# Two transformer layers in split float32: the split weights in one tile, with the token-major pairs 128 bytes further on

## The chip, the cores and the metric

The kernel runs on 1 core of a Trainium2 chip. The metric is the device time of one execution in microseconds (us). Three runs of the kernel before took 845.11 to 846.7 us, median 845.73.

## The reference

Two post-norm layers work on `x` of 256 tokens by 1024 channels, all in float32. Cut to what matters:

```python
def hybrid_mixer(x, ...):
    proj = jnp.einsum('bsd,de->bse', x, w_in)          # 12 parts side by side
    y_a = sliding_window_attention(a_q, a_k, a_v, sinks, slopes_a)
    y_b = gated_short_conv(b_h, b_b, b_c, conv_w)
    y_c = moba_attention(c_q, c_k, c_v, slopes_c)
    merged = (sigmoid(g_a) * (y_a @ w_br_a) + sigmoid(g_b) * (y_b @ w_br_b)
              + sigmoid(g_c) * (y_c @ w_br_c))
    return merged @ w_out

def reference(x, ...):
    for l in range(2):
        x = layer_norm(ALPHA * x + hybrid_mixer(x, ...), ln1_g[l], ln1_b[l])
        ffn = (silu(x @ w_gate) * (x @ w_up)) @ w_down
        x = layer_norm(ALPHA * x + ffn, ln2_g[l], ln2_b[l])
    return x
```

## The kernel before, in words

**Split arithmetic.** Every matrix product is made of three matmuls on numbers split in two: a high part, which is the value rounded to the type `float32r`, and a low part, which is what is left. High times high, high times low and low times high are added up in PSUM. ScalarE writes the high part (`wh`) and VectorE subtracts to get the low part (`wl`); for weights this is `parts` (L182 and L183 in the profile), for activations the helper `halve` (L272 and L273).

**Pieces and the ring.** The host packs all weights into 140 pieces of 128 partitions by 2048 columns (8 KB per partition, 1 MB). `load` (L154) brings a piece into one of three raw buffers on SP's queue. `open_splits` gives it a place and `split_piece` adds its split, two parts of 1024 columns. The place is one of four slots of a ring, a tile for `wh` and a tile for `wl` from the pool `wts`, which is taken in turn; three pieces of a layer's cycle go into a tile that stands free at that moment, `wA` or `wB` (the table `place`). `take` makes the planner finish a piece's split in its order of emission, `drop` gives the slot back.

**Two orders of operands.** In a matmul one operand stands still in the array (it is loaded by a LDWEIGHTS) and the other moves through it.
- `whole` works on a block of 256 output channels in channel-major order: `trio` lets the weights stand still (128 x 128) and moves 256 tokens of `xx` past them. A piece is two accumulators `acc` of 24 matmuls. `branch` (`br`) and `merge` (`gc`) use `trio` in the same way, `br` with `y` instead of `xx`.
- `half_pair` works on two pieces for half of the tokens in token-major order: `tokens` lets 128 tokens of `xx` stand still and moves 256 weight columns past them (two runs of 128 columns, 4 KB apart). Its accumulators are `hp`, 24 matmuls per piece and half, 48 per pair and half. It is used where the tokens of one half are ready before those of the other: around a norm. Its pieces are 2 and 3 of layer 0 (`qkv_pair`), the first four of the FFN in each layer (`ffn_pair`), and the first four of layer 1 (`qkv_pair`).
- `project` (`pr`, mostly 512 columns) and `cv` move weights too, in runs of 512 columns.

**Addresses.** All big tiles start at a multiple of 256 bytes in their partition, also `wh`, `wl`, `mx` and the hidden tiles. `xx` and `y` start 48 words (192 bytes) further on (`AHEAD`), and every slice of them that a matmul reads keeps this remainder. So does a small tile of 16 words behind each, which brings the next tile back to a multiple of 256.

**Order.** A planner (`Plan`) emits the work of ScalarE and VectorE in the order of its estimated times, while the loops emit TensorE's. Engines PE, DVE, ACT and SP keep the order of emission. The order in a layer is: q, k and v blocks; attention in eight rounds, between blocks of the other projections, each round with scores (`s`), transposes (`tp`) and mixing (`yp`); `branch`, `merge`; the output projection with the first norm, in whose shadow the pairs of the FFN run; 18 blocks of the FFN (`whole`, 864 matmuls); the down projection with the second norm, in whose shadow the pairs of the next layer run.

```python
def tokens(acc, wv, k, h, src, first, last):
    wh, wl = wv
    t = slice(h * P, (h + 1) * P)
    mm(acc, src[k][:, 0, t], wh, first, False)
    mm(acc, src[k][:, 0, t], wl, False, False)
    mm(acc, src[k][:, 1, t], wh, False, last)

def trio(acc, wh, wl, src, first, last):
    mm(acc, wh, src[:, 0, :], first, False)
    mm(acc, wh, src[:, 1, :], False, False)
    mm(acc, wl, src[:, 0, :], False, last)
```

Of the kernel before, what the change touches and what calls it, by code (L numbers as in the profile page):

```python
# [9 lines left out]
FT = mybir.dt.float32  # L10
FR = mybir.dt.float32r
# [5 lines left out]
P = 128  # L17
D = 1024
S = 256
L = 2  # L20
KD = D // P
# [3 lines left out]
PIECE = 2048  # L25
CHUNK = 1024
RING = 4
RAWS = 3
N_IN, N_BR, N_OUT, N_FF, N_DN = 27, 6, 4, NF, NF // 2
PER_LAYER = N_IN + N_BR + N_OUT + N_FF + N_DN  # L30
# [3 lines left out]
FAR = 1.0e30  # L34
LINE = 64
EARLY = 8
AHEAD = 48


# [77 lines left out]
def trunk(ctx: ExitStack, tc: tile.TileContext, x, first, w, sinks, conv, ln, out):  # L117
    nc = tc.nc
    pool = lambda name, bufs, **k: ctx.enter_context(tc.tile_pool(name=name, bufs=bufs, **k))
    const = pool("const", 1)  # L120
    raws = pool("raws", RAWS)
    wts = pool("wts", RING)
    keep = pool("keep", 1)
    work = pool("work", 2)
    ps = pool("ps", 4, space=bass.MemoryType.PSUM)
    ctx.enter_context(tc.manual_schedule(engines={ENG.PE, ENG.DVE, ENG.Activation, ENG.SP}))
# [3 lines left out]
    place = {}  # L130
# [4 lines left out]
    total = L * PER_LAYER  # L135
    slots = [0.0] * RING
    spare, ready, chunks, raw, landed, rawfree = {}, {}, {}, {}, {}, {}
    pos = {"load": 0, "split": 0, "take": 0}

    def cut(j):  # L140
# [3 lines left out]
    def load(hold=False):  # L144
        j = pos["load"]
        if j >= total:
            return
        pos["load"] += 1
        if j:
            raw[j] = raws.tile([P, PIECE], FT, name="raw")  # L150
            if hold:
                nc.vector.memset(raw[j][:, 0:1], 0.0)
            for s in cut(j):
                nc.sync.dma_start(raw[j][:, s], w[j - 1][:, s])  # L154
        landed[j] = max(landed.get(j - 1, 3.5), rawfree.get(j - RAWS, 0.0) + 2.0) + 3.0
        open_splits()
# [4 lines left out]
    def open_splits():  # L161
        while pos["split"] < pos["load"]:
            j = pos["split"]
            if j in place:
                if place[j] not in spare:
                    return
                t = spare.pop(place[j])
                both = keep.tile([P, 2, PIECE], FR, tag=place[j], name="w" + place[j])
                ready[j] = both[:, 0, :], both[:, 1, :]
            else:  # L170
                if not slots:
                    return
                t = slots.pop(0)
                ready[j] = wts.tile([P, PIECE], FR, name="wh"), wts.tile([P, PIECE], FR, name="wl")
            pos["split"] += 1
            if j:
                split_piece(j, max(t, landed[j]))
# [7 lines left out]
    def split_piece(j, t, n=CHUNK):  # L185
        def last(task):
            rawfree[j] = task.ready
            load()

        need = T.pe + 5.2 * (j - pos["take"])  # L190
        ss = [slice(c, c + n) for c in range(0, PIECE, n)]
        chunks[j] = [T.add(parts(j, s), t - (1.5 if len(cut(j)) > 1 and not i else 0.0), max(need - t, 0.0) + 0.001 * i, last if s.stop == PIECE else None)
                     for i, s in enumerate(ss)]

    def take():
        j = pos["take"]
        pos["take"] += 1
        T.run()
        T.finish(*chunks.pop(j))
        return j  # L200

    def drop(j):
        if j in place:
            if j % PER_LAYER == N_IN + N_BR + N_OUT:
                spare["B"] = T.pe
        else:
            slots.append(T.pe)
        del ready[j]
        open_splits()
# [90 lines left out]

    xx = keep.tile([P, AHEAD + KD * 2 * S], FR, name="xx")
    xx = xx[:, AHEAD:].rearrange("p (k a s) -> p k a s", k=KD, a=2)
    xk = [xx[:, k] for k in range(KD)]
    rest = keep.tile([P, LINE - AHEAD], FT, name="rest")
    nc.gpsimd.memset(rest, 0.0)


    both = keep.tile([P, KD, 2 * S], FT, tag="A", name="first")
    rest = keep.tile([P, LINE - AHEAD], FT, name="rest2")
    nc.gpsimd.memset(rest, 0.0)  # L310
# [12 lines left out]
    spin = ps.tile([P, P], FT, tag="o", name="spin")  # L323
    for i in range(EARLY):
        nc.tensor.matmul(spin, idle, idle, start=True, stop=True)
# [292 lines left out]
    def mixer_tiles():  # L618
        mix = keep.tile([P, 18 * S + 4 * (S + 2) + 56], FT, tag="mix", name="mix")
        aq, ak, av, cq, ck, cv = [  # L620
            mix[:, lo * S:hi * S].rearrange("p (k s) -> p k s", k=k)
            for lo, hi, k in ((0, 4, 4), (4, 5, 1), (5, 6, 2), (6, 10, 4), (10, 14, 4), (14, 18, 2))]
        return aq, ak[:, 0, :], av, cq, ck, cv, mix[:, 18 * S:18 * S + 4 * (S + 2)].rearrange("p (k s) -> p k s", k=4)
# [26 lines left out]
    for l in range(L):  # L650
        aq, ak, av, cq, ck, cv, up = tiles = mix or mixer_tiles()
        y = keep.tile([P, AHEAD + 12 * 2 * S], FR, tag="A", name="y")
        y = y[:, AHEAD:].rearrange("p (b k a s) -> p b k a s", b=3, k=4, a=2)
        nc.gpsimd.memset(up[:, :, 0:2], 0.0)
# [39 lines left out]
        for n in range(2):  # L694
            j = take()
# [47 lines left out]
            for part in (conv_h, conv_c, conv_b):  # L743
                whole(part)

        gs = keep.tile([P, 2, KD, S], FT, tag="B", name="gs")
        sums, raw_gates, sig = {}, {}, {}

        def gates(b):
# [66 lines left out]
        merge()  # L816
        spare["A"] = spare["B"] = T.pe
        open_splits()

        hid, last_f = [], {f: [] for f in range(NF)}  # L820
# [127 lines left out]
```

## Time and profile before

| what | value |
|---|---|
| median of three runs | 845.73 us (845.11 to 846.7) |
| the profiled execution | 849.06 us |
| its span, first to last instruction | 847.3 us |
| TensorE busy | 834.6 us, 99% |
| VectorE, ScalarE, GpSimd busy | 583.3, 456.5, 56.9 us |
| mean granted clock of TensorE | 0.997 |
| read from memory | 153.11 MB, 182 GB/s over the span |

The profile shows one execution. A duration of a matmul in it runs from its start to its modelled end, and matmuls overlap (a `hp` matmul lasts some 280 ns while the next starts some 118 ns later), so the rate is not read from mean durations. It is read from the chain of waits, where a row is an unbroken stretch of one kind of matmul with its time and its count.

### The profile page before, as it was taken

To read this page: it belongs to the slowest core of one execution; us is meant where nothing else is said; L and a number is where in the kernel's file an instruction comes from. 1 tells how busy PE (TensorE), PEld (TensorE's weight loads), DVE (VectorE), ACT (ScalarE), POOL (GpSimd) and SP (SyncE) were. 2 spreads that over 40 slices of the span, in tenths; PEclk is the share of its full clock that TensorE was granted. 3 is DMA by queue.
4 is the path that set the end of the run, shared out by engine and by line. 5 is a ranking of instruction groups with operands and counts; after the bars stand their busy time and mean duration, and the time that the engine had idled before them with its cause. 6 is when DMAs were issued, how large, how long until landed. Compare 5 with 4: busy or idle time off the path is not lost.

```text
span 847.3 us, 15513 instructions
## 1 busy us (share of the span) xinstructions
PE 834.6 (99%) x6390; PEld 793.7 (94%) x6390; DVE 583.3 (69%) x980; ACT 456.5 (54%) x809; POOL 56.9 (7%) x81
## 2 busy tenths in 40 slices
PE   8999999999999999999999999999999999999996
PEld 7989989999899999988899899999998999999885
DVE  5588999577967566545657799966688666556435
ACT  6667677645525445434347776865563345444320
POOL 2003500000110000000000044000000100000000
PEclk9999999999999999999999999999999999999998
DMA  8753445556655555556336424554646465555511
GB/s 302 295 186 114 150 153 202 198 196 199 249 199 197 184 174 193 199 191 235 121 107 243 149 100 142 207 209 166 222 161 245 171 224 196 199 172 184 193 50 50
DMA packets 23318, 155.15 MB, mean 183 GB/s; under 512 B 2608, under 2 KB 2896, under 8 KB 5840
## 3 DMA queue, kind: packets, MB, share of 16 engines
q1 hardware_dynamic: 22032, 149.96, 50.1%
q0 software_dynamic: 1216, 4.22, 1.7%
q8 instruction: 50, 0.82, 0.4%
q14 instruction: 20, 0.16, 0.1%
HBM read 153.11 MB, written 1.05 MB: 182 GB/s over the span
## 4 chain that ended last, share of the span: by engine, by line
PE 94%; DMA 3%; DVE 1%; ACT 1%; issue 0%; SPq 0%; POOLq 0%; POOL 0%; DVEq 0%; ACTq 0%
PE acc L254 46%; PE pr L254 17%; PE hp L254 9%; PE br L254 8%; PE gc L254 5%; PE cv L254 3%; PE tp L267 2%; PE s L254 2%; DMA gb<-ln 1%; DMA first<-first 1%; PE yp L490 1%; DMA raw<-w 1%; PE yp L492 0%; DVE xtok L518 0%; ACT xa L272 0%
## 5 line engine op out<-in xcount | busy, mean ns | idle before, releaser
L254 PE MATMUL acc<-xx,wh 128*128 128x256 f32 x2304 | 405.7, 280 | 2.1 <-ACT wh L272 2.1
L183 DVE TENSOR_TENSOR wl<-raw,wh 128x1024 fp32r<-128x1024 f32 x266 | 322.4, 1229 | 108.7 <-ACT wh L182 108.0
L182 ACT ACTIVATE wh<-raw 128x1024 fp32r<-128x1024 f32 x266 | 274.2, 1053 | 194.4 <-PE acc L254 79.6
L254 PEld LDWEIGHTS acc<-xx,wh 128*128 128x128 f32 x2304 | 350.2, 188 | 3.4 <-ACT wh L272 2.6
L254 PE MATMUL acc<-xx,wl 128*128 128x256 f32 x1152 | 321.9, 279 | 0.7 <-DVE wl L273 0.4
L254 PEld LDWEIGHTS acc<-xx,wl 128*128 128x128 f32 x1152 | 218.8, 190 | 1.5 <-DVE wl L273 0.8
L254 PE MATMUL hp<-wh,xx 128*128 128x256 f32 x384 | 70.9, 282 | 0.0
L279 DVE TENSOR_TENSOR g<-g,acc 128x256 f32<-128x256 f32 x72 | 30.1, 418 | 57.5 <-PE acc L254 57.1
L254 PE MATMUL br<-y,wh 128*128 128x256 f32 x384 | 67.9, 281 | 0.0
L254 PE MATMUL pr<-wh,hidA 128*128 128x512 f32 (+1 forms) x216 | 60.7, 366 | 0.0
L254 PEld LDWEIGHTS hp<-wh,xx 128*128 128x128 f32 x384 | 59.6, 188 | 0.0
L254 PEld LDWEIGHTS br<-y,wh 128*128 128x128 f32 x384 | 58.9, 190 | 0.0
L254 PE MATMUL br<-y,wl 128*128 128x256 f32 x192 | 54.0, 281 | 0.0
L254 PE MATMUL hp<-wl,xx 128*128 128x256 f32 x192 | 53.6, 279 | 0.0
L254 PE MATMUL gc<-xx,wh 128*128 128x256 f32 x256 | 45.3, 281 | 0.0
L254 PEld LDWEIGHTS pr<-wh,hidA 128*128 128x128 f32 x216 | 39.1, 189 | 6.6
L254 PE MATMUL pr<-wh,hidB 128*128 128x512 f32 (+1 forms) x144 | 41.8, 366 | 0.0
L254 PE MATMUL pr<-wl,hidA 128*128 128x512 f32 (+1 forms) x108 | 39.5, 366 | 0.0
L254 PEld LDWEIGHTS gc<-xx,wh 128*128 128x128 f32 x256 | 39.3, 190 | 0.0
L254 PEld LDWEIGHTS hp<-wl,xx 128*128 128x128 f32 x192 | 36.1, 188 | 0.0
L254 PEld LDWEIGHTS br<-y,wl 128*128 128x128 f32 x192 | 36.0, 188 | 0.0
L254 PE MATMUL gc<-xx,wl 128*128 128x256 f32 x128 | 36.0, 281 | 0.0
(134 smaller groups left out, 959.5 us busy)
## 6 DMA issues: line engine op xcount, KB each, us to landing
raw<-w SPq DMA_DIRECT2D x136, 1024.0 KB, 5.0
gb<-ln POOLq DMA_DIRECT2D x8, 512.0 KB, 5.1
raw<-w SPq DMA_DIRECT2D x6, 512.0 KB, 8.8
first<-first SPq DMA_DIRECT2D x4, 512.0 KB, 5.7
xtok<-x SPq DMA_DIRECT2D x2, 512.0 KB, 6.3
out<-xtok SPq DMA_DIRECT2D x3, 256.0 KB, 2.0
out<-xtok SPq DMA_DIRECT2D x2, 128.0 KB, 1.8
cw<-conv POOLq DMA_DIRECT2D x1, 12.0 KB, 5.5
```

Of the source, the lines that this page charges most:

```text
L182: return [act(n) + (lambda: nc.scalar.activation(wh[:, s], raw[j][:, s], AF.Copy),), dve(n) + (lambda: nc.vector.tensor_sub(wl[:, s], raw[ ...
L183: dve(n) + (lambda: nc.vector.tensor_sub(wl[:, s], raw[j][:, s], wh[:, s].bitcast(FT)),)]
L254: nc.tensor.matmul(acc, a, b, start=start, stop=stop)
L267: nc.tensor.transpose(tp[:, i, :], src(i), ident)
L279: return [dve(n) + (lambda: nc.vector.tensor_mul(dst, a, b),)]
L490: nc.tensor.matmul(yp[los[a], :], v[:, 0, vsel[a]], pts[a][:, 0:2, :], start=True, stop=False)
```

## The change

The pool `wts` goes. In its place stands one tile `ring` with four slots of 2 x 2048 + 32 words, `wh` and `wl` of a piece side by side in a slot. A counter (`turns`) picks the slot. A piece of the list `pairs`, which are the pieces that `half_pair` reads, starts 32 words (128 bytes) past a multiple of 64 words (256 bytes); all others start at a multiple of 256 bytes. The kept tiles `wA` and `wB` are 64 words longer, so that the first piece of the FFN (in `wB`, a pair) can start 32 words in; `gs`, which shares its memory with `wB`, gets the same length.

```diff
@@ -119,8 +120,8 @@
     raws = pool("raws", RAWS)
-    wts = pool("wts", RING)
     keep = pool("keep", 1)
+    ring = keep.tile([P, RING * (2 * PIECE + HALF)], FR, name="ring")
     work = pool("work", 2)
@@ -135,6 +136,9 @@
     slots = [0.0] * RING
     spare, ready, chunks, raw, landed, rawfree = {}, {}, {}, {}, {}, {}
+    turns = [0]
+    ffn = N_IN + N_BR + N_OUT
+    pairs = [2, 3] + [l * PER_LAYER + j for l in range(L) for j in range(ffn, ffn + 4)] + [PER_LAYER + j for j in range(4)]
     pos = {"load": 0, "split": 0, "take": 0}
@@ -165,13 +169,17 @@
                 t = spare.pop(place[j])
-                both = keep.tile([P, 2, PIECE], FR, tag=place[j], name="w" + place[j])
-                ready[j] = both[:, 0, :], both[:, 1, :]
+                both = keep.tile([P, 2 * PIECE + LINE], FR, tag=place[j], name="w" + place[j])
+                lo = HALF * (j in pairs)
+                ready[j] = both[:, lo:lo + PIECE], both[:, lo + PIECE:lo + 2 * PIECE]
             else:
                 if not slots:
                     return
                 t = slots.pop(0)
-                ready[j] = wts.tile([P, PIECE], FR, name="wh"), wts.tile([P, PIECE], FR, name="wl")
+                lo = turns[0] % RING * (2 * PIECE + HALF)
+                turns[0] += 1
+                lo += (lo % LINE + HALF * (j in pairs)) % LINE
+                ready[j] = ring[:, lo:lo + PIECE], ring[:, lo + PIECE:lo + 2 * PIECE]
@@ -743,7 +751,8 @@
-        gs = keep.tile([P, 2, KD, S], FT, tag="B", name="gs")
+        gs = keep.tile([P, 2 * KD * S + LINE], FT, tag="B", name="gs")
+        gs = gs[:, :2 * KD * S].rearrange("p (b k s) -> p b k s", b=2, k=KD)
```

`HALF` is 32 and `LINE` is 64, in words of 4 bytes. Every engine has the same instructions in the same order in both kernels; only the name of the weights' tile differs (`ring` for `wh` and `wl`). What a split waits for differs: with a tile per slot it waited for the release of the tile, and in one tile it waits for the last instructions that touch its own region.

## Rows read from the trace of the kernel before

**Rows 1.** The page, part 1: busy us, share of the span, instructions
```profile
PE 834.6 (99%) x6390; PEld 793.7 (94%) x6390; DVE 583.3 (69%) x980; ACT 456.5 (54%) x809; POOL 56.9 (7%) x81
```

**Rows 2.** Waits of PE: us in total, times, longest us
```profile
PE acc L254 <- ACT wh L272: 2.1, 2, 1.4
PE spin L325 <- DVE xtok L322: 1.1, 1, 1.1
PE tp L267 <- DVE xtok L518: 0.6, 1, 0.6
PE tp L267 <- DVE prob L455: 0.5, 1, 0.5
PE acc L254 <- DVE wl L273: 0.4, 2, 0.2
PE acc L254 <- DVE raw L152: 0.2, 1, 0.2
```

**Rows 3.** Chain that ended last, `acc`, `br`, `gc`: start us, us, what, count
```profile
34.45 11.31 PE acc L254 x96
...
46.47 4.10 PE acc L254 x36
...
99.70 9.54 PE acc L254 x84
...
157.94 33.92 PE br L254 x288
191.86 22.61 PE gc L254 x192
...
261.34 4.10 PE acc L254 x36
...
265.65 97.52 PE acc L254 x828
...
448.51 1.42 PE acc L254 x12
...
450.25 10.90 PE acc L254 x96
...
461.86 4.10 PE acc L254 x36
...
479.32 5.47 PE acc L254 x48
...
564.44 1.38 PE acc L254 x12
...
681.26 97.52 PE acc L254 x828
```

**Rows 4.** The same chain, the pairs `hp`
```profile
237.17 8.48 PE hp L254 x72
...
246.09 2.83 PE hp L254 x24
...
252.63 5.66 PE hp L254 x48
...
445.78 2.73 PE hp L254 x24
```

**Rows 5.** Stretches: from:to us, length, busy us per engine, PEclk, DMA share, GB/s
```profile
266.00:362.00 96.00, 96.00 (x818) 96.00 (x817) 59.15 (x87) 46.05 (x69) 0.00 (x0) 1.00 0.55 188
446.00:448.00 2.00, 2.00 (x20) 2.00 (x19) 1.79 (x3) 1.88 (x3) 0.00 (x0) 1.00 0.78 254
```

**Rows 6.** Waits of all engines, the two of the weight splits
```profile
DVE wl L183 <- ACT wh L182: 108.0, 86, 5.7
ACT wh L182 <- PE acc L254: 79.6, 38, 2.4
```

**Rows 7.** The page, part 6: a load of a piece, KB each, us to landing
```profile
raw<-w SPq DMA_DIRECT2D x136, 1024.0 KB, 5.0
```

More of the change, by code (lines that the diff above doesn't have):

```diff
@@ L36 @@
 EARLY = 8
+HALF = 32
 AHEAD = 48
```

## The prediction

> **What bounds the kernel now.** I read the page's busy times first. TensorE is busy 834.6 of 847.3 us, and VectorE, ScalarE and GpSimd have slack [rows 1]. TensorE's waits come next: all of them together are 4.9 us [rows 2]. So nothing but TensorE's own pace can be worth much, and the chain of waits, which is 94% TensorE, is read for that pace: each of its rows is an unbroken stretch of matmuls, and its time divided by its count is the time of one.
>
> The reader is to see that one form, 128x256, runs at two paces. The matmuls of whole column blocks (`acc`) take 9.54 / 84 = 113.6 ns in one stretch, 113.9 in the stretch of 36 in front of the FFN loop, and 97.52 / 828 = 117.8 ns in the FFN loop, in both layers [rows 3]. `br` (33.92 / 288) and `gc` (22.61 / 192) take 117.8 [rows 3]. The token-major pairs (`hp`) take 8.48 / 72 = 117.8 and 2.83 / 24 = 117.9, and in one stretch alone 2.73 / 24 = 113.8 [rows 4]. The chain has 17 rows of `hp` with 672 matmuls, and 16 of these rows are at the long pace; of its 39 rows of `acc`, 31 are at 115 ns or less. [...]
>
> The pace is kept for a whole stretch and can differ in the next, with something else between (transposes, scores, the other order of operands): 36 `acc` at 113.9, two transposes, and 828 `acc` at 117.8 [rows 3]. The 828 of a loop pass through all four slots of the ring four times at one pace, so the slot is not the reason either.
>
> **What the addresses are.** In `whole` the weights stand still and start at a multiple of 256 bytes, and `xx` moves and starts 192 past one: the moving operand lies 64 bytes below the stationary one, modulo 256. In the pairs `xx` stands still (192) and the weights move (0): 64 above. The change puts the moving weights of the pairs at 128, which is 64 below 192: the relation that `whole` has now. That relation gives no guarantee, as the FFN loop and `br` and `gc` have it and run at 117.8 [rows 3]. But it is the one in which most stretches settle at the short pace, while in the pairs' present relation one of 17 does.
>
> **The change part by part.** (1) The pairs' addresses. Of the 672 matmuls in the 17 rows, 24 are at the short pace already [rows 4], so 648 can gain 117.8 - 113.6 = 4.2 ns each: 2.7 us if all turn, nothing if none does. All of it lies on TensorE, the bound, with no cover. Which stretches turn? Four of 72 follow a projection or `acc` without transposes between, 288 matmuls; the rest follow 2 to 12 transposes. `acc` has both outcomes behind transposes: two transposes lead to the long pace at 265.65 and at 681.26, three to the short pace at 450.25 [rows 3]. The pairs have 144 matmuls behind two transposes, which I leave at the long pace by that row, and I count four fifths of the other 528, as 31 of 39 rows of `acc` are short: 422, less the 24 that have it, some 400. 400 x 4.2 = **1.7 us gained**. The ends of this term are 0 and 2.7.
>
> (2) What follows the pairs. An `acc` stretch starts in whatever position the pairs leave. 36 `acc` behind long-pace pairs run at 113.9, and 12 `acc` behind the one short-pace stretch at 1.42 / 12 = 118 [rows 3, 4]. These are few: 12, 36, 36 and 12 in the four places, and 96 behind the last of them. Were all 180 now short to turn long, it would cost 0.8 us; were the 12 to turn short, they would give 0.05. I take 0, as the entry from pairs of the same relation has no row. The loops of 828 lie behind two transposes and those 36 `acc`; as long as the 36 stay short, what enters the loop is what enters it now, so I take no change for the loops; the end is 828 x 4.2 = 3.5 us gained for each loop (a rival, below).
>
> (3) The ring as one tile. The same instructions stand on every engine in the same order. What moves is what the splits wait for: a split of 1024 columns waits for the last reader of its own region, where it waited for the last reader of the whole tile. ScalarE's splits now wait 79.6 us for `acc` and VectorE's subtractions 108.0 us for ScalarE, in 38 and 86 waits [rows 6]; these are waits for a slot to come free, with splits a whole ring ahead of TensorE. Releasing the first half of a piece earlier lets a split start up to half a piece earlier, 24 x 0.118 = 2.8 us. TensorE waits for `wh` and `wl` only in the helper's lines L272 and L273, that is for the first block, 2.1 and 0.4 us, before the ring is ever reused [rows 2], so this is worth 0. What it could reach is the 1.1 us that TensorE waits for VectorE in transposes of `xtok` and `prob` [rows 2]: up to 1.1 gained if these vanish, and as much lost if one more appears because a subtraction that waits for a region holds VectorE's queue with a softmax or a norm behind it. I take 0 and keep +-1.1.
>
> (4) The padding (128 bytes more in each slot, 256 in each kept tile) adds no instruction and moves no other tile off its multiple of 256, so 0; a step that reads from the padded tile has the same number of elements. Loads stay 136 of 1 MB, 5.0 us each to land, on SP's queue in the same order [rows 7].
>
> Sum: 1.7 us gained. The profiled execution took 849.06 us with a span of 847.3, so it would take 847.4; the median of the runs, 845.73, stands 3.3 us below it, and the same gain gives **844.0 us**. About 0.2% (1.7 us) is what a measurement of this kernel can tell from no change, so the forecast stands on that border.
>
> [...] What the rows show first: two paces of one form at the full clock [rows 3, 5], so something beside the number of columns sets the pace. [...]
>
> **The rivals.** *A. The address is not what matters* (chance 0.20). The pace is set at the entry of a stretch, by where it falls in time, and the pairs are slow because of what stands before them: transposes and projections, which stay. For it: the `hp` stretch at 445.78 is short at the old address [rows 4], and `acc` is long in 828 at the good one [rows 3]. Against it: 1 of 17 rows against 31 of 39. Then 845.7, give or take the 1.1 of (3).
>
> *B. The FFN loops are carried along* (0.14). The pairs stand right in front of both loops, with 36 `acc` and two transposes between. If another position enters the loop and it settles at the short pace, 828 x 4.2 = 3.5 us more for each: with the forecast's 1.7, 840.5 for one loop and 837.0 for both. For it: 96 `acc` behind three transposes settle short after a long stretch of 12 [rows 3, 4], so what stands before the transposes matters. Against: both layers enter alike today and both come out long.
>
> *C. Short stretches behind the pairs turn long, and it is slower* (0.10). In layer 1 the pairs feed the attention part directly: 96 and 36 `acc` at 450.25 and 461.86, and 624 more up to 566 that run at 113.6 to 115. If the entry changes and all 756 settle long, 756 x 4.2 = 3.2 us lost, and with pairs that gain nothing the time is 848.9. It decides from about 400 matmuls more turned long than short (1.7 / 4.2 ns). Against it: layer 0 enters its attention part at 117.8 (34.45, 11.31 / 96) and layer 1 at 113.5, and behind the first scores both are at 113.9 [rows 3], so the scores and transposes in between seem to wipe out the entry.
>
> **How the numbers follow.** The forecast has 0.56, with 240 to 648 of the pairs turned, 1.0 to 2.7 us: 844.7 to 843.0. It ends over 0.2% faster in a little more than half of its cases (0.33), and within 0.2% in the others (0.23). A is within 0.2% (0.18) but for 0.01 at either side; B is faster (0.14); C is slower in 0.09 and within 0.2% in 0.01. So faster 0.48, same 0.42, slower 0.10. The range reaches down past one loop of B to 839.0 (one loop 3.5, all pairs 2.7, and some of (3)) and leaves out most of the case of both loops; upward it reaches 847.2, half of C, and leaves out the rest.
>
> **What would show it.** In the profile after, the rows of `hp` in the chain should read about 8.2 for 72, 5.45 for 48 and 2.73 for 24, in at least half of their matmuls; the rows of 36 `acc` stay at 4.10 and the loops at 97.52; `br` at 33.92 and `gc` at 22.6; and TensorE's waits stay near 4.9 us. All rows of `hp` at 117.8 would make (1) wrong and A right; a loop at 94.1 us would be B; rows of 84 `acc` at 9.9 instead of 9.54 would be C.

## The result and the profile after

The changed kernel takes 839.39 us (median of 4 runs, 839.11 to 840.19), the kernel before, measured beside it, 846.22 (845.11 to 846.88). The ratio is 0.9916 with a 95% interval of 0.9901 to 0.9932: faster by 0.84%, or 6.8 us. The predicted time was 844.0 us in a range from 839.0 to 847.2, so the time stands just inside its lower end, 0.4 us from it. The profiled execution has a span of 837.7 us, against 847.3 before.

TensorE's busy time answers to [rows 1]: it fell by 7.1 us, most of the 9.6 by which the span fell.

```profile
PE 827.5 (99%) x6390; PEld 787.3 (94%) x6390; DVE 584.6 (70%) x980; ACT 457.7 (55%) x809; POOL 56.8 (7%) x81
```

So the gain is one of pace, and the chain of waits of the changed kernel says where. Its rows (start us, us, what, count) answer to [rows 3, 4]; all these matmuls have the form 128x256.

```profile
33.62 10.90 PE acc L262 x96
...
156.14 33.92 PE br L262 x288
190.06 22.61 PE gc L262 x192
...
235.37 8.48 PE hp L262 x72
...
244.28 2.74 PE hp L262 x24
...
256.61 2.83 PE hp L262 x24
259.44 4.24 PE acc L262 x36
263.90 93.86 PE acc L262 x828
...
428.30 5.46 PE hp L262 x48
...
444.47 11.31 PE acc L262 x96
...
670.82 4.24 PE acc L262 x36
675.28 93.86 PE acc L262 x828
```

Read them against the rows before, by time over count:

| stretch | before, ns each | after, ns each | us in the two layers together |
|---|---|---|---|
| FFN loop, 828 `acc`, both layers | 117.8 | 93.86 / 828 = 113.4 | -7.3 |
| pairs `hp`, 672 | 24 of them short | 168 of them short | -0.6 |
| 36 `acc` ahead of the loop, both layers | 113.9 | 4.24 / 36 = 117.8 | +0.3 |
| 96 `acc` behind the pairs | 117.8 in layer 0, 113.5 in layer 1 | 113.5 and 117.8 | 0 (-0.4 and +0.4) |
| `br` and `gc` | 117.8 | 117.8 | 0 |

These add to -7.6 us. The medians differ by 6.8, with an interval (0.0099 and 0.0068 of 846.2) of 5.8 to 8.4 us. The remaining 2.0 us of the 9.6 between the two spans lie in the start and in single waits that vary from execution to execution: the first run below has the loops, `br` and `gc` at the paces of the kernel before and a span of 845.0, 2.3 us shorter. Some 0.7 of these 2.3 us are a matter of pace too: its first 72 pairs and the 96 `acc` of layer 0 came out short, without any shift. So the -0.4 us of layer 0 in the table is no sign of the change.

The 168 short pairs are the 24 at 244.28, the two rows of 48 at 428.30 and 434.09, and two more rows of 24; none of the four blocks of 72 turned. The pairs, which alone were shifted, gave little. The loops, whose weights stand at multiples of 256 bytes as they did, gave nearly all.

The clock has no part in it: the granted clock reads 1.00 in a stretch of either pace in [rows 5], with TensorE busy throughout. This is the loop of layer 0 after the change by windows (from and to, length, busy us per engine, granted clock, DMA share, GB/s): again 1.00, and TensorE busy 90.00 of 90.00 us, at the other pace.

```profile
266.00:356.00 90.00, 90.00 (x796) 90.00 (x795) 58.95 (x84) 45.30 (x68) 0.00 (x0) 1.00 0.57 199
```

The waits of TensorE answer to [rows 2] (us in total, times, longest).

```profile
PE acc L262 <- ACT ring L280: 1.2, 2, 0.8
```

Those of the weight splits, in the view of all engines, answer to [rows 6].

```profile
DVE ring L191 <- ACT ring L190: 86.4, 49, 5.5
...
ACT ring L190 <- PE pr L262: 51.1, 15, 8.9
```

ScalarE's splits waited 79.6 us for `acc` before; that wait is gone from the view. VectorE's wait for ScalarE fell from 108.0 to 86.4 us. The finer waits of the one tile do what the third step said. TensorE, which waited 2.1 and 0.4 us in all for split weights [rows 2], got next to nothing from it.

### The profile page after: what moved, and what is told of

It is laid out like the page before. It is cut to its first block, busy times and chain, and to the rows that moved or that the text cites. A ratio compares the mean times of both kernels' runs of the same rounds, so it can differ in the third digit from the quotient of the medians.

```text
span 837.7 us, 15533 instructions
## 1 busy us (share of the span) xinstructions
PE 827.5 (99%) x6390; PEld 787.3 (94%) x6390; DVE 584.6 (70%) x980; ACT 457.7 (55%) x809; POOL 56.8 (7%) x81
## 4 chain that ended last, share of the span: by engine, by line
PE 92%; DVE 4%; DMA 1%; POOL 1%; issue 0%; ACT 0%; SPq 0%; POOLq 0%
PE acc L262 43%; PE pr L262 20%; PE hp L262 9%; PE br L262 8%; PE gc L262 5%; PE cv L262 3%; PE tp L275 2%; PE s L262 1%; DMA first<-first 1%; PE yp L498 1%; DVE ring L191 1%; DVE xa L281 1%; PE yp L500 0%; POOL hh L740 0%; DVE prob L467 0%
## 5 line engine op out<-in xcount | busy, mean ns | idle before, releaser
L262 PE MATMUL acc<-xx,ring 128*128 128x256 f32 x3456 | 405.0, 278 | 1.4 <-ACT ring L280 1.2
L262 PEld LDWEIGHTS acc<-xx,ring 128*128 128x128 f32 x3456 | 399.1, 189 | 2.8 <-ACT ring L280 1.7
L191 DVE TENSOR_TENSOR ring<-raw,ring 128x1024 fp32r<-128x1024 f32 x266 | 322.2, 1229 | 87.1 <-ACT ring L190 86.4
L190 ACT ACTIVATE ring<-raw 128x1024 fp32r<-128x1024 f32 x266 | 274.7, 1053 | 104.6 <-PE pr L262 51.1
L262 PE MATMUL hp<-ring,xx 128*128 128x256 f32 x576 | 70.3, 281 | 0.0
L262 PEld LDWEIGHTS hp<-ring,xx 128*128 128x128 f32 x576 | 68.2, 189 | 0.1
L262 PE MATMUL br<-y,ring 128*128 128x256 f32 x576 | 68.2, 281 | 0.0
L262 PEld LDWEIGHTS br<-y,ring 128*128 128x128 f32 x576 | 68.0, 189 | 0.0
L262 PE MATMUL pr<-ring,hidA 128*128 128x512 f32 (+1 forms) x324 | 66.2, 366 | 0.0
L262 PEld LDWEIGHTS pr<-ring,hidA 128*128 128x128 f32 x324 | 55.9, 189 | 9.9
L511 DVE SCALAR_TENSOR_TENSOR xtok<-xtok,pr 128x512 f32<-128x512 f32 (+1 forms) x17 | 11.1, 655 | 23.4 <-PE pr L262 23.3
```

The costliest lines, as they stand in the source:

```text
L190: return [act(n) + (lambda: nc.scalar.activation(wh[:, s], raw[j][:, s], AF.Copy),), dve(n) + (lambda: nc.vector.tensor_sub(wl[:, s], raw[ ...
L191: dve(n) + (lambda: nc.vector.tensor_sub(wl[:, s], raw[j][:, s], wh[:, s].bitcast(FT)),)]
L262: nc.tensor.matmul(acc, a, b, start=start, stop=stop)
L511: dve(n) + (lambda: nc.vector.scalar_tensor_tensor(r, r, ALPHA, acc, op0=OP.mult, op1=OP.add),)] + [
```

## The experiments

The theory after this result: the pace of a stretch is set where TensorE enters it and then kept; the shift of the pairs matters because another position now enters the FFN loops. Its first rival is that the ring as one tile, with its finer waits, makes the gain; its second, that the addresses of a stretch's own operands decide over its pace, as the first step of the prediction held. In all runs but the first three, one extra matmul of a chosen number of columns (called a kick) stands ahead of a stretch: it reads operands that the matmuls there read and writes into the accumulator that the next one overwrites, so the result is the same. A kick changes no address; it changes what TensorE does just before it enters what follows, and adds some 0.1 us (0.11 to 0.12 in run 4).

| run | edit | us | kernel before, measured beside it | FFN loops, us |
|---|---|---|---|---|
| 1 | the change without its shift | 847.1 (10 runs) | 846.95 | 97.52, 97.52 |
| 2 | the shift with the pool of before | 840.45 (4) | 846.95 | 93.86, 93.86 |
| 3 | shift of the 8 pieces ahead of the loops alone | 842.74 (1) | 846.95 | 93.86, 93.86 |
| 4 | before, 8 kicks in each loop | 845.95 (1) | 846.95 | mixed |
| 5 | the change, kicks in `br` and `gc` | 839.06 (1) | 847.24 | 93.86, 93.86 |
| 6 | the change, kicks ahead of the pairs | 844.86 (1) | 847.24 | 97.53, 97.53 |
| 7 | the change, one kick in each loop | 846.95 (1) | 847.24 | 816 in 96.20, twice |
| 8 | the change, ten kicks | 835.31 (4) | 846.37 | 768 in 87.09, twice |
| 9 | before, six kicks | 835.82 (4) | 846.37 | 768 in 87.07, twice |
| 10 | run 9 and kicks ahead of the unshifted pairs | 836.3 (4) | 846.75 | 768 in 87.07, twice |
| 11 | before, 28 kicks in the pairs | 849.82 (1) | 845.04 | 97.52, 97.52 |
| 12 | the change, the same 28 kicks | 849.14 (1) | 845.04 | 97.53, 97.53 |

### Runs 1 and 2: the tile or the shift

Run 1 keeps the one tile and shifts nothing:

```diff
-    pairs = [2, 3] + [l * PER_LAYER + j for l in range(L) for j in range(ffn, ffn + 4)] + [PER_LAYER + j for j in range(4)]
+    pairs = []
```

> The changed kernel with an empty list of pairs: the ring is one tile, with the padded slots and the finer waits, but every piece starts at a multiple of 256 bytes. Theory 'entry' (the 128 bytes move the position in time at which the pairs' matmuls start, and with it what enters the FFN loops): both loops of 828 back at 97.5 us and the pairs at 117.8 ns, so some 846 us, within 1 us of the kernel before. Theory 'ring' (one tile, slots side by side, earlier release of half a piece): the loops at 93.9 us and some 839.5 us without any shift.

Run 2 takes the kernel before with its pool, one tile for each slot, and the shift:

```diff
-                ready[j] = wts.tile([P, PIECE], FR, name="wh"), wts.tile([P, PIECE], FR, name="wl")
+                lo = turns[0] % RING * (2 * PIECE + HALF)
+                turns[0] += 1
+                lo = (lo % LINE + HALF * (j in pairs)) % LINE
+                slot = wts.tile([P, 2 * PIECE + HALF], FR, name="slot")
+                ready[j] = slot[:, lo:lo + PIECE], slot[:, lo + PIECE:lo + 2 * PIECE]
```

> The kernel before with a tile from a pool for each slot, wh and wl side by side in it, at the same addresses as in the changed kernel, and the pairs shifted by 128 bytes: the addresses of the change without its one tile and its finer waits. Entry: the same as the changed kernel, both loops at 93.9 us, 839 to 840 us. Ring: loops at 97.5 us and some 846 us.

The chain of run 1:

```profile
260.17 4.09 PE acc L262 x36
264.49 97.52 PE acc L262 x828
```

A wait of run 1 (us in total, times, longest):

```profile
DVE ring L191 <- ACT ring L190: 86.7, 49, 5.7
```

The chain of run 2:

```profile
260.28 4.24 PE acc L263 x36
...
264.74 93.86 PE acc L263 x828
```

Run 1 is the kernel before in its time (ratio 1.0002, 0.9992 to 1.0011), though VectorE's wait for ScalarE is as short as in the changed kernel, 86.7 us against 86.4. Run 2 has the gain (0.9927, 0.9907 to 0.9947) and the paces of the changed kernel, with a pool. So the shift makes the gain and the tile none; the first rival falls.

### Run 3: which pairs

```diff
-    pairs = [2, 3] + [l * PER_LAYER + j for l in range(L) for j in range(ffn, ffn + 4)] + [PER_LAYER + j for j in range(4)]
+    pairs = [l * PER_LAYER + j for l in range(L) for j in range(ffn, ffn + 4)]
```

> The changed kernel with the shift for the eight FFN pieces alone (pieces 2 and 3 of layer 0 and the first four of layer 1 stay at multiples of 256). Entry: the loops stand right behind the FFN pairs, so both stay at 93.9 us; the stretch of 96 matmuls in front of layer 1's attention goes back from 117.8 to 113.5 ns (0.4 us better than the changed kernel), the one in layer 0 back from 113.5 to 117.8; the time within 1 us of 839.4. If instead the loops need the other pairs too, one of them is at 97.5 us and the time some 843 us.

```profile
35.73 11.31 PE acc L262 x96
...
267.30 93.86 PE acc L262 x828
...
448.26 10.90 PE acc L262 x96
```

Only the pairs right ahead of the loops are shifted, and both loops are short. The 96 `acc` behind the other pairs went back to what they were before, long in layer 0 and short in layer 1. In layer 1 this is a sign: they are short without the shift of their pairs (the kernel before, runs 1, 3, 4 and 9) and long with it (the changed kernel, runs 2, 5 and 7). In layer 0 it is none: they take 10.90 without the shift in runs 1, 4 and 9. So the loops, and layer 1's 96 `acc`, hear of the shift in the pairs just ahead of them and of no other. (One run; its first pairs began at 22.35 us instead of 20.25, which is most of its 3.3 us above the changed kernel.)

### Run 4: kicks at addresses that do not change

```diff
+KICK = {l * PER_LAYER + N_IN + N_BR + N_OUT + f: n for l, ns in enumerate(
+    ((128, 64, 192, 32, 224, 96, 240, 160), (64, 192, 32, 224, 96, 240, 160, 128))) for f, n in zip(range(5, 21, 2), ns)}
...
+        if n:
+            nc.tensor.matmul(accs[0][0][:, :n], wh[:, 0, 0, :], xk[0][:, 0, :n], start=True, stop=True)
```

> The kernel before, all addresses as they were, with 8 short extra matmuls in each FFN loop, one in front of every second block (32 to 240 columns wide, on the block's first operands, into the accumulator that the block's first matmul then overwrites). Entry: the pace within a loop changes at some of these points, from 117.8 to 113.5 ns or back, at unchanged addresses, and stays until the next; each one costs some 0.05 to 0.2 us itself. Theory 'relation' (the pace belongs to the pair of addresses, or is fixed for the loop by something else than the entry): all blocks stay at 117.8 ns, and the time rises by 1 to 3 us.

```profile
265.80 11.36 PE acc L257 x96
277.19 10.98 PE acc L257 x96
288.25 10.91 PE acc L257 x96
299.18 11.40 PE acc L257 x96
...
679.92 10.99 PE acc L257 x96
```

A row of 96 matmuls takes 10.9 to 11.0 us at the short pace and 11.3 to 11.4 at the long one, the kick included. In layer 0, 128 columns ahead of the first row leave it long, 64 turn it short, 192 leave it short, 32 turn it long. In layer 1, 64 columns in the place of the 128 turn the first row short. So the matmuls of one loop, at the addresses that they had before, run at either pace, and the kick at the entry chooses which, for all of the 96 matmuls up to the next kick. The second rival does not hold for the loops.

What the width of a kick chooses is not a longer or shorter delay. Four kicks of layer 0, in the view by time (start us, us, what):

```profile
276.99 0.20 PE L389 MATMUL acc<-xx,wh 128*128 128x64 f32 x1
288.00 0.25 PE L389 MATMUL acc<-xx,wh 128*128 128x192 f32 x1
299.00 0.18 PE L389 MATMUL acc<-xx,wh 128*128 128x32 f32 x1
310.42 0.27 PE L389 MATMUL acc<-xx,wh 128*128 128x224 f32 x1
```

From one start to the next lie a kick and 96 matmuls. The first two distances are 11.01 and 11.00 us, and 96 x 113.4 ns are 10.89; the third is 11.42, and 96 x 117.8 ns are 11.31. So kicks of 64, 192 and 32 columns cost 0.11 to 0.12 us each. What it is at the entry that the width changes, these views do not show.

### Runs 5, 6 and 7: other stretches, and the loops undone

From here the kick is a function, called ahead of the piece that the table names (a pair of a number and a half stands for pairs).

```diff
+    def kick(acc, j, a, b):
+        n = KICK.pop(j, 0)
+        if n:
+            nc.tensor.matmul(acc, a, b[..., :n], start=True, stop=True)
```

Run 5, in `br` (pieces 25, 27, 95, 97), `gc` (29, 99) and the 48 `acc` ahead (22, 92):

```diff
+KICK = {22: 64, 25: 96, 27: 64, 29: 192, 92: 96, 95: 192, 97: 64, 99: 64}
```

> The changed kernel with four short extra matmuls in each layer between the last mixing and the output projection, a stretch of 528 (48 acc, 288 br, 192 gc) that has run at 117.8 ns in every kernel so far: layer 0: 64 columns at the 48 acc, 96 at the second branch, 64 at the third, 192 at gc; layer 1: 96, 192, 64, 64. Entry: as in the loops, 64 or 96 columns take the stretch from 117.8 to 113.5 ns and 192 leaves a short stretch short, so at least one of the parts of each layer is short; all 1056 short would be 4.4 us. What 64 columns do to a stretch that is short already is open. Relation: all parts at 117.8 and the time up by 0.5 us.

Run 6, ahead of the four blocks of 72 pairs:

```diff
+KICK = {(2, 0): 64, (37, 0): 64, (70, 0): 64, (107, 0): 64}
```

> The changed kernel with one extra matmul of 64 columns in front of each of the four stretches of 72 pair matmuls. Entry: these 288 go from 117.8 to 113.5 ns (1.2 us); what follows them is entered elsewhere and may turn either way, the FFN loops too (3.6 us lost for each that turns long). Relation: nothing changes but 0.3 us of extra matmuls.

Run 7, 12 matmuls behind the start of each loop:

```diff
+KICK = {42: 32, 112: 32}
```

> The changed kernel with one extra matmul of 32 columns in front of the first whole block of each FFN loop (in the kernel before 32 columns took a short stretch to the long pace). Entry: both loops of 828 back to 117.8 ns, the rest as in the changed kernel, some 846.5 us: the whole gain of the change gone at its own addresses. If the gain lies elsewhere than in the loops the time stays at 839.5 us.

Run 5:

```profile
157.09 10.88 PE br L264 x96
168.01 11.38 PE br L264 x96
...
190.89 21.81 PE gc L264 x192
...
578.62 10.93 PE br L264 x96
589.58 11.39 PE br L264 x96
```

Run 6:

```profile
235.22 8.25 PE hp L264 x72
...
258.68 4.24 PE acc L264 x36
263.13 97.53 PE acc L264 x828
```

Run 7:

```profile
265.71 96.20 PE acc L264 x816
```

Run 5 has `br` and `gc`, which no address change had touched, at both paces. Its rows also show what I can't yet say: 64 columns made one `br` long and left two stretches long, where in run 4 they made two short. The outcome depends on what a kick meets, and not on its width alone.

Run 6 got what the first step of the prediction wanted: all four blocks of 72 at 8.25 and, in the rows behind them, 2.74 for 24 and 5.46 for 48, so that all 672 pairs are short. And it lost the gain: the loops fell back to 97.53, and the time to 844.86. It also shows that 36 `acc` at the long pace do not make the loop short by themselves, as 4.24 stands ahead of a short loop in the changed kernel and ahead of a long one here.

Run 7 leaves the pairs as the change made them and puts both loops back with 32 columns: 846.95, against 847.24 before. The gain of the change is the loops.

### Runs 8 and 9: every entry put right, with the shift and without

Run 8 is the changed kernel, run 9 the kernel before:

```diff
+KICK = {(2, 0): 64, (37, 0): 64, (70, 0): 64, (107, 0): 64, 22: 64, 92: 64, 42: 64, 43: 192, 112: 64, 113: 192}
```

> The changed kernel with ten extra matmuls: 64 columns ahead of the four blocks of 72 pairs, of the 48 acc behind the mixing in both layers, and of the second FFN piece; 192 columns ahead of the third FFN piece. If the pace is set where a stretch is entered and any extra matmul may reset it: pairs as in the run with extra matmuls ahead of the pairs (-1.6 us against the change), the 48 acc, 288 br and 192 gc of both layers at 113.4 instead of 117.8 ns (rows 33.9 and 22.6 become 32.7 and 21.8, 528 matmuls x 4.4 ns = -2.3 us in each layer), both FFN loops back at 113.4 ns (some 92.5 for 816), and some 0.1 us paid for each extra matmul: 839.4 - 1.6 - 4.6 + 0.9 = 834.1 us. If the addresses of the operands decide over the pace, the extra matmuls change nothing behind themselves: loops 97.5 long as in that run, br and gc at 33.9 and 22.6, some 845 us.

```diff
+KICK = {22: 64, 92: 64, 42: 64, 43: 192, 112: 64, 113: 192}
```

> The kernel before, no address changed, with six extra matmuls (64 columns ahead of the 48 acc behind the mixing and of the second FFN piece in both layers, 192 columns ahead of the third FFN piece). If the shift of 128 bytes matters only by what it leaves at the entry of a stretch: FFN loops at 113.4 ns without any shift (-3.6 us each), br and gc with the 48 acc at 113.4 ns (-2.3 us in each layer), pairs unchanged at 8.48 per 72: 846.5 - 7.2 - 4.6 + 0.5 = 835.2 us. If the loops need the pairs' shift to be short: they stay at 97.5 or fall back after the extra matmuls, 841 to 847 us.

Run 8:

```profile
157.07 32.64 PE br L264 x288
...
234.17 8.25 PE hp L264 x72
...
269.36 87.09 PE acc L264 x768
```

Run 9:

```profile
157.44 32.64 PE br L256 x288
...
234.51 8.48 PE hp L256 x72
...
270.07 87.07 PE acc L256 x768
```

Both beat both kernels: run 8 takes 835.31 us (ratio 0.9872, 0.9855 to 0.9888), 11.1 below the kernel before and 4.1 below the 839.39 of the changed one, which was measured at another time; run 9 takes 835.82 (0.9877, 0.9859 to 0.9895). In run 9 no address is moved, the loops are short (768 at 113.4 ns), and `br` and `gc`, which the change left long, are short too: 33.92 to 32.64 and 22.61 to 21.76, with the 48 `acc` ahead 5.85 to 5.54, in all 2.4 us for each layer, of which the kick ahead takes back 0.2. Six extra matmuls give more than the shift does. With them, what the shift still adds (all pairs short in run 8) is 0.5 us between the medians, with overlapping runs (835.04 to 835.79, 834.38 to 837.54), which can't be told from nothing.

### Runs 10 to 12: does the address matter at all to the pairs?

Run 6 turned all pairs at their new addresses. Run 10 tries it at the old ones, in run 9:

```diff
-KICK = {22: 64, 92: 64, 42: 64, 43: 192, 112: 64, 113: 192}
+KICK = {(2, 0): 64, (37, 0): 64, (70, 0): 96, (107, 0): 32, 22: 64, 92: 64, 42: 64, 43: 192, 112: 64, 113: 192}
```

> The run before with no shift, and an extra matmul ahead of each of the four blocks of 72 pairs at their old addresses: 64 columns at two of them, 96 at the third, 32 at the fourth. If only the entry sets the pace: at least two of the four blocks read 8.25 instead of 8.48, with the rows of 24 and 48 behind them partly at 2.74 and 5.46, and 0.1 us paid for each extra matmul: some 0.3 us for each block that turns, 835.0 us. If the old relation of the addresses (moving operand 64 bytes above the stationary one) keeps pairs long, as the prediction held: all four stay at 8.48 and the rows behind them at 117.8 ns, 836.2 us. FFN loops, br and gc short as in that run either way, if their own extra matmuls hold.

```profile
234.84 8.56 PE hp L256 x72
...
418.24 8.55 PE hp L256 x72
...
643.94 8.58 PE hp L256 x72
```

None of these three turned; with the extra matmul in it, a block reads 8.55 to 8.58 here and 8.25 in run 6. (The fourth block is not in this chain; its matmuls start 117.8 ns apart.) Not all of the expectation came true: behind two of the blocks a row of 24 is short, 2.73 us at 243.84 and at 652.95. The time, 836.3, is no better than that of run 9 (835.3 to 836.89 against 834.38 to 837.54). Since four tries are few, runs 11 and 12 put the same kick ahead of each of the 28 groups of 24 pairs, in the kernel before and in the changed one:

```diff
+KICK = {(j, h): (64, 96, 32, 128)[(i + h) % 4] for i, j in enumerate([2, 3, 37, 38, 39, 40, 70, 71, 72, 73, 107, 108, 109, 110]) for h in range(2)}
```

> The kernel before, no shift, with an extra matmul ahead of every group of 24 pairs (28 of them, of 64, 96, 32 or 128 columns in turn). If the entry alone sets the pace, a good part of the 28 groups of 24 run at 113.4 to 114 ns (2.73 us for 24), as 4 of the 8 extra matmuls in the first layer's FFN loop led to the short pace: 10 to 20 of 28. If the relation of the addresses keeps the pairs long, as in the run before this one, at most 4 of 28 are short (one of 17 rows was, without extra matmuls). Each extra matmul costs some 0.1 us.

> The same 28 extra matmuls in the changed kernel, pairs 128 bytes past multiples of 256. If the entry alone sets the pace: as many short groups as in the run with the old addresses, give or take 5. If the relation of the addresses decides whether pairs can be short: 20 or more of 28 short here, against at most 4 there.

Run 11, the old addresses:

```profile
236.19 2.92 PE hp L256 x24
...
258.31 2.82 PE hp L256 x24
```

Run 12, the new ones:

```profile
236.46 2.83 PE hp L264 x24
239.35 2.88 PE hp L264 x24
```

With the kick in it, a group of 24 reads 2.78 to 2.84 at the short pace and 2.88 to 2.92 at the long one. At the old addresses 2 of 28 are short (258.31 and 674.73), at the new ones 16 of 28. The same place with the same 32 columns reads 2.92 and 2.83 in the rows that stand first in the two fences. So the address does matter: behind a kick a group of pairs rarely settles at the short pace at the old address, and more often than not at the new one. Twenty and more were expected if the address decided alone; 16, with 12 long at the same addresses, say that both have a part. The 28 are not 28 separate trials: in both runs the eight groups of the FFN have the same outcomes in layer 1 as in layer 0, which leaves 20 different places, 1 of them short at the old addresses and 11 at the new. The expectation took 4 of 8 from run 4; in its first loop 3 of 8 kicks led to the short pace. (Both runs stand 4 to 5 us above the kernel before: the loops are long in both, and 28 kicks are paid.)

The old address does not forbid the short pace, though. These are the `acc` that run straight into the first block of 72, and the start of that block, in the chain from 18 to 24 us. Run 4, old addresses:

```profile
17.93 2.95 PE acc L257 x26
20.88 3.17 PE hp L257 x28
```

The changed kernel:

```profile
17.98 2.27 PE acc L262 x20
20.25 3.77 PE hp L262 x32
```

The `acc` run at 113 ns in both. In run 4 the pairs, unshifted, go on at 113 for the whole block (8.17 us for 72); in the changed kernel they go on at 118. By the starts of the matmuls, the block keeps the pace of the `acc` ahead of it wherever it is unshifted and has no kick (long in the kernel before and run 3, short in runs 1, 4 and 9) and takes the other one wherever it is shifted (long behind short in the changed kernel and runs 2 and 5, short behind long in run 7). The joint ahead of the loops, where the pairs hand over to the 36 `acc`, shows the shift at work too: behind long pairs these are short at the old addresses (4.09 or 4.10 us, 10 of 10 in the kernel before and runs 1, 4, 9 and 10) and long at the new ones (4.24, 10 of 10 in the changed kernel and runs 2, 3, 5 and 7). So the shift works at the joint between two orders of operands: it changes which pace the next stretch takes, even where the pairs themselves keep theirs.

## Why the prediction was right, and where it was not

**The size of the gain came from a rival.** The forecast of 844.0 was 4.6 us too high. The range held the time because it reached down past one loop of rival B; what happened is B with both loops, priced at 837.0 with all of the forecast's 1.7 us for the pairs. That the time lies in the range is luck: the prediction said that it leaves out most of this case, to which B gave 0.14 with that of one loop. The mechanism that B named, "another position enters the loop and it settles at the short pace", is what runs 3, 4 and 7 show, as far as the entry decides; that it is the position in time was not shown.

**The step that failed is the second**, "so I take no change for the loops". It rested on the 36 `acc` ahead of the loop staying short, and gave no row for that: they went from 4.10 to 4.24. (Their pace alone does not decide either, by run 6.) Nor was the argument against B any: "both layers enter alike today and both come out long" says that the two will do alike, not that they will stay. They did alike, and both turned. With 1656 matmuls in the loops against 672 pairs, the larger term hung on the entry, which the change was sure to move; it deserved a chance near one half, with 7.3 us to win.

**The first step was right in part and mis-sized.** That the address matters to the pairs is shown by runs 11 and 12, 2 against 16 of 28. That the new relation itself brings them to the short pace is not: without a kick the shift turned the first block long behind short `acc` as well as short behind long. But the 1.7 us for some 400 turned pairs were 0.6 for 144. The 144 behind two transposes that I left long did stay long (the row at 256.61 is one of them). Of the other 528, four fifths were counted, a share borrowed from `acc`. Of the 240 among them behind other transposes 168 are short, 0.7, near that share; the 288 in the four blocks of 72, which follow a projection or `acc` without transposes between, did not turn at all. They were counted with the rest, although the trace had no pairs at the short pace behind such an entry; run 6 shows that it can be had there, with one kick each. The count behind the step was off by one: the chain has 16 rows of `hp` with these 672 matmuls, of which 15 are long. And the share of 31 of 39 rows is one of rows, many of them of 12 matmuls: by matmuls, 1392 of the 3334 `acc` in that chain are at the short pace.

**What tells the address from the entry.** No row of the kernel before does. Runs 11 and 12 differ in the shift and in the ring, and of the two only the shift moved a pace in runs 1 and 2; the count of short groups then differs by 14 of 28. So the addresses of the operands have a part in the pace of the pairs. Whether it is the distance between the two operands or the place of the moving one alone was not told apart, as the stationary `xx` stayed where it was. A shift of 64 or 192 bytes was not tried.

**The third and fourth steps were right.** Run 1 measures the tile, its finer waits and the padding together: 0.15 us between the medians, against the 1.1 that were allowed. Splits wait less (VectorE for ScalarE 86.7 us instead of 108.0), and TensorE gains next to nothing by it: its waits for the split weights are 1.8 and 0.4 us in run 1, and were 2.1 and 0.4 before.

**The other rivals.** A (the address does not matter) is wrong by runs 11 and 12, but half of its argument is right: the entry is what decides over the loops. C (short stretches turn long) happened in small: 36 `acc` in both layers and 96 in layer 1, 0.7 us, against 0.4 in layer 0, which run 1 has without the shift. The 84 `acc` in the attention part stayed at 9.54, so the entry is indeed wiped out there.

**What stays open.** Why an entry leads to one pace or the other, and whether it is the moment of entry or something else that a kick leaves behind; it brings a load of weights of its own (run 4 has 6406 matmuls and 6406 loads of weights, the kernel before 6390 of each, and 16 kicks are the difference). The rows give starts to 10 ns, kicks of 32, 64 and 192 columns cost 0.11 to 0.12 us each in run 4, and a kick of 64 columns had all three outcomes: long to short, short to long, long kept. I can say that the entry decides, and not predict for a new place which kick turns it; run 8 needed two kicks at each loop to be safe, and its 96 `acc` behind the pairs came out long.

## What to carry to other kernels

When TensorE is busy throughout at one granted clock (1.00 here in stretches of both paces), divide the time of each stretch in the chain by its count, by form: if one form has two values, the difference may be a gain that no wait will show, here 11 us of 846. Look for it at the entry of the longest stretch, and try one extra short matmul of 32 to 192 columns there before you move addresses or tiles: it costs some 0.1 us and is easy to undo. Try several widths: in the first loop of run 4, three of eight led to the short pace. And when a change touches a short stretch right ahead of a long one, price the long one by its two values first.

## What the runs showed of the hardware

A stream of 128x256 matmuls has two paces at a granted clock of 1.00, 113.4 ns (93.86 / 828) and 117.8 (97.52 / 828), and no row of 96 or more of them in these runs reads between 114.5 and 117.8. The short one is half of the 226.8 ns (57.14 / 252) that the 512-column matmuls of `pr` take. The pace holds for 828 matmuls through four slots of the ring, and one extra matmul of 64 columns changes it, in either direction (`acc` to short in run 4, `br` to long in run 5). The kicks in the loop of run 4 cost 0.11 to 0.12 us at 32, 64 and 192 columns. Where the two operands stand matters as well: of 28 groups of pairs with the same kicks, 2 are short with the moving operand at a multiple of 256 bytes and 16 with it 128 bytes further, the stationary one at 192 in both. Behind long pairs 36 `acc` take 4.10 us in the first case and 4.24 in the second, 10 of 10 each.
